# Weight sums of a hybrid block: later stores in the projection, two of twelve groups made in the score stage

## The chip, the cores and the metric

The kernel runs on one core of a Trainium2 chip. The metric is the device time of one execution, in microseconds (us). A core has TensorE (PE, matmuls; its weight loads are PEld), VectorE (DVE), ScalarE (ACT), GpSimd (POOL) and SyncE (SP). Each executes its instructions in the order in which they stand in its own stream, and waits for the others through semaphores. Transfers (DMA) are issued by SyncE, and in one place of this kernel by ScalarE, and run on 16 DMA engines.

## The reference

One layer of a hybrid block on x, 512 tokens of 2048 features in f32:

```python
xn = _rmsnorm(h, norm_mix[l])
y = xn @ w_in[l]
o_gdn = _gdn_group(y[..., :GDN_COLS], ...)      # 8 heads of 128, chunks of 64
o_rwkv = _rwkv_group(y[..., GDN_COLS:], ...)    # 16 heads of 64
mixed = jnp.concatenate([o_gdn, o_rwkv], axis=-1)
h = h + mixed @ w_out[l]
h = h + _cross_attention(_rmsnorm(h, norm_xattn[l]), _rmsnorm(mem, norm_mem[l]),
                         wq, wk, wv, wo)        # 4 heads, 256 memory tokens
hn = _rmsnorm(h, norm_mlp[l])
h = h + jnp.square(jax.nn.relu(hn @ mlp_w_up[l])) @ mlp_w_down[l]   # 2048 -> 8192 -> 2048
return _rmsnorm(h, norm_final)
```

Both recurrent groups solve, for each chunk of 64 tokens, a triangular system (GDN by its formula, RWKV-7 because the kernel computes its scan in chunks too).

## The kernel before, in words

**Stages.** In order: the projection (product tiles py, with the recurrent heads and the key and query products kp and kq of the cross-attention among them) to about 1240 us; the value and output products of the attention (vp, vo) to about 1330; the out projection (op) to 1483; the score stage (sc) to about 1573; the attention's end (at); the MLP's way up (mxu, mgu, mmu) to about 2300; its way down (mxd, mgd, mmd) to the end.

**f32 products.** A weight tile (wraw, w, kqr) of 128x1024 is split into a high part (whi, kqh: a ScalarE cast to a rounded f32) and a low part (wlo, kql: VectorE subtracts). A product is then three matmuls: high x high, high x low, low x high.

**Weight sums.** The MLP multiplies its weights in 2x2 blocks by Strassen-like (Winograd) schemes, which need sums of blocks. Of the down weights w_dm there are 16 groups (e, m); 12 of them (GROUPS) are made beforehand: for each column range, four pieces a21, a22, a11, a12 are loaded, VectorE makes four sums s1 to s4 in place, and each is stored to a DRAM buffer Sd (sd_s in the profile), 2048 columns in all. The MLP loads them from there. `presum` yields these steps for one piece, `presums` goes through the list todo of groups piece by piece, and `ahead` starts it within the projection: NSET = 1 set of four tiles (ds), PIECE = 410 columns, until kp number 15 is done. What is then left in todo, `remaining` and `leftover` make within the MLP, 512 or 256 columns at a time.

**Who sets the order.** The projection and the MLP are ordered by a planner in the kernel's own Python. A chain is a generator that yields operations; each has a rank (`chain(gen, rank)`, the sums' rank is 2 for SyncE and PRANK for the others). `run` takes, again and again, the next operation of the chains by an estimated start (`start`) and the rank, and `issue` emits it: all operations of the planned stages are therefore emitted by one line, L256. A Lane names the engine and carries two numbers of nanoseconds. The first, `wait`, is added to the moment at which the operands are assumed ready, for the operation itself (it is then put later in its engine's stream). The second, `margin`, is added to the assumed landing of the operation's own transfer (whatever uses its result is put later). The lanes of SyncE that matter are SY (none), SL (wait 6000), SM (margin 2500) and the one for the pieces' loads (margin 5000):

```python
SL, SM = Lane(nc.sync, "SP", wait=6000.0), Lane(nc.sync, "SP", margin=2500.0)
t = max(t, x + op[7][0] + (0.0 if by == eng else CROSS))          # start
t, eng = max(state["dma"] + 700, t + 2900) + slack[1], "DMA"      # issue
```

These numbers move nothing at run time; they change only where an instruction stands.

**The triangular inverses.** `rwkv(j)` runs for j = 0 to 7, a pair of RWKV heads each ("head j" from here on), `gdn(h)` for eight GDN heads. Both call `inverse_blocks`: TensorE's products (pg and the like for RWKV, pkk for GDN) are stored to DRAM by SyncE (ndri, ndgi), the 16x16 diagonal blocks are loaded again in another layout (sr, sgi), 33 GpSimd operations invert them (15 steps of two, and copies), the inverses are stored to DRAM (bg16T/bg16U for RWKV, bg8T/bg8U for GDN) and loaded again through the lane SM (r and E for RWKV; gk, gqn for GDN). `inverse_levels` then combines the blocks on TensorE, beginning with the products ri0x to ri7x, or gi0x to gi7x. The small weights lw of `rwkv`, for the product pW, are loaded through SM as well. The matmuls of py that stand between pg (or pkk) and ri_x (or gi_x) in TensorE's stream are called cover below; "wide" is one of 512 columns, "narrow" a smaller one. Other transfers on SyncE in this stage: mixd, gE (from mg and gB), gqd, lg, and the projection's weights, wraw, 512 KB each.

**The score stage.** It, like all that lies between the planned stages, is ordered by the framework's scheduler. A loop over g (2) and n2 (8) makes 16 steps. Each loads two halves of a key tile (kqr, 2 x 256 KB), splits it (kqh, kql; two sets of buffers) and does 24 matmuls of 512 columns on 4 accumulators. In the first six steps `second` makes the high and low parts of the state (hh, hl), `softmax` and `turned` stand between later steps.

Of the kernel before, what the change touches and what calls it, by code (L numbers as in the profile page):

```python
# [9 lines left out]
F32 = mybir.dt.float32  # L10
F32R = mybir.dt.float32r
AF = mybir.ActivationFunctionType
ALU = mybir.AluOpType
# [4 lines left out]
P = 128  # L18
T = 512
M = 256  # L20
# [53 lines left out]
def build(tc, I, out):  # L74
    nc = tc.nc
    V, S, GP, PE = nc.vector, nc.scalar, nc.gpsimd, nc.tensor
# [4 lines left out]
    ps = es.enter_context(tc.tile_pool(name="ps", bufs=1, space=PSUM))  # L81
    pw = es.enter_context(tc.tile_pool(name="pw", bufs=1))
# [45 lines left out]
    def split(src, hi, lo, gain=None):  # L128
        if gain is None:
            S.copy(hi, src)  # L130
            V.tensor_tensor(out=lo, in0=src, in1=hi.bitcast(F32), op=ALU.subtract)  # L131
        else:
            S.activation(hi, src, AF.Copy, scale=gain)
            V.scalar_tensor_tensor(out=lo, in0=src, scalar=gain, in1=hi.bitcast(F32),
                                   op0=ALU.mult, op1=ALU.subtract)

    NWR, NWS, NY = 3, 3, 4
# [66 lines left out]
                return self.key, nm, getattr(self.eng, nm), a, k, out, aps, self.slack  # L204
            return op

    SL, SM = Lane(nc.sync, "SP", wait=6000.0), Lane(nc.sync, "SP", margin=2500.0)
    DV, AC, GS, TE, SY = (Lane(e, k) for e, k in ((V, "DVE"), (S, "ACT"), (GP, "POOL"), (PE, "PE"), (nc.sync, "SP")))

    def cost(op):  # L210
# [142 lines left out]
    KQd = [pd.tile([P, 1024], F32, name=f"kqd{i}", tag=f"kqd{i}") for i in range(16)]  # L353
# [25 lines left out]
    for n in range(2, NIN):  # L379
# [5 lines left out]
    A11, A21, A22, A12 = range(4)  # L385
    Sd = {(e, m, j): pd.tile([P, 2048], F32, name=f"sd{e}_{m}_{j}", tag=f"sd{e}_{m}_{j}")
          for e, m in GROUPS for j in ("s1", "s2", "s3", "s4")}
    NSET, PIECE, PRANK = 1, 410, 5
    todo = list(GROUPS)
    upto = {}  # L390

    def presum(e, m, c, n, d, Q=None):
        Q = Q or SY
        LD = Lane(nc.sync, "SP", margin=5000.0)
        tt = lambda o, a, b, op=ALU.subtract: DV.tensor_tensor(out=o, in0=a, in1=b, op=op)
        src = I["w_dm"][e, m]
        a11, a21, a22, a12 = b = [x[:, 0:n - c] for x in d]
        for i in (A21, A22, A11, A12):
            yield LD.dma_start(b[i], src[i][:, c:n])
        for j, op in (("s1", tt(a22, a21, a22, ALU.add)), ("s3", tt(a21, a11, a21)),  # L400
                      ("s2", tt(a11, a22, a11)), ("s4", tt(a12, a12, a11))):
            yield op
            yield Q.dma_start(Sd[e, m, j][:, c:n], op[5])
            upto[e, m, j] = upto.get((e, m, j), 0) + n - c

    def presums(d, width, stop):
        while todo and not stop():
            e, m = todo.pop(0)
            for c in range(0, 2048, width):
                if c and stop():  # L410
                    todo.insert(0, (e, m))
                    return
                yield from presum(e, m, c, min(c + width, 2048), d)

    hk = [("w", I["wk"][n][:, h * 1024:(h + 1) * 1024]) for n, h in kpo]
    wq += [("m", m) for m in mem4[:3]] + hk[:1] + [("m", mem4[3])] + hk[1:]
# [1146 lines left out]
    def second(n):  # L1563
        hi, lo = act_tile(f"hh{n}"), act_tile(f"hl{n}")
        split(hres[n], hi, lo, col("norm_xattn", n))
        hh_.append(hi)
        hl_.append(lo)
# [66 lines left out]
    def softmax(t):  # L1634
        g, pts, probs = turn[0]
        mx, nb, sm = (pl.tile([P, 2], F32, tag=f"{x}1", name=f"{x}{g}_{t}", bufs=4) for x in ("mx", "nb", "sm"))
        V.tensor_reduce(out=mx, in_=pts[t].rearrange("p (e m) -> p e m", m=M), axis=AX.X, op=ALU.max)
        V.tensor_scalar(out=nb, in0=mx, scalar1=nrcol[:, t:t + 1], scalar2=None, op0=ALU.mult)
        prs = [prob[g * 8 + t * 2 + e][:, 0:M] for e in range(2)]
        for e, pr in enumerate(prs):  # L1640
            S.activation(pr, pts[t][:, e * M:(e + 1) * M], AF.Exp, bias=nb[:, e:e + 1], scale=rcol[:, t:t + 1],
                         accum_out=sm[:, e:e + 1])
        V.reciprocal(out=sm, in_=sm)
        for e, pr in enumerate(prs):
            V.tensor_scalar(out=pr, in0=pr, scalar1=sm[:, e:e + 1], scalar2=None, op0=ALU.mult)
        probs += prs

    def turned():
        g, _, probs = turn.pop(0)
        for e in range(2):  # L1650
            for mt in range(2):
# [4 lines left out]
                S.copy(phi[kk], pt)  # L1656
                V.tensor_tensor(out=plo[kk], in0=pt, in1=phi[kk].bitcast(F32), op=ALU.subtract)

    for g in range(2):
        banks = (("mm", 2), ("mg", 2), ("mg", 2), ("mm", 2)), (("scr", 1), ("scg", 1), ("mx", 2), ("mx", 2))  # L1660
        pts = [psb(f"sc{g}_{t}", *banks[g][t]) for t in range(4)]
        for n2 in range(8):
            cnt[0] += 1
            raw = pw.tile([P, 1024], F32, tag="wraw", name=f"kqr{cnt[0]}", bufs=NWR)
            for i in range(2):
                nc.sync.dma_start(raw[:, i * 512:(i + 1) * 512], KQd[2 * n2 + i][:, g * 512:(g + 1) * 512])
            wh = pw.tile([P, 1024], F32R, tag="whi", name=f"kqh{cnt[0]}", bufs=NWS)
            wl = pw.tile([P, 1024], F32R, tag="wlo", name=f"kql{cnt[0]}", bufs=NWS)
            split(raw, wh, wl)
            if g == 0 and n2 < 6:  # L1670
                second(2 * n2 + 4)
                second(2 * n2 + 5)
            its = [(i, t) for i in range(2) for t in range(4)] if n2 < 7 else [(i, t) for t in range(4) for i in range(2)]
            for i, t in its:
                n = 2 * n2 + i
                w1, w2 = wh[:, i * 512:(i + 1) * 512], wl[:, i * 512:(i + 1) * 512]
                a1, a2 = hh_[n][:, t * P:(t + 1) * P], hl_[n][:, t * P:(t + 1) * P]
                mm(pts[t], a1, w1, start=(n == 0), stop=False)
                mm(pts[t], a1, w2, start=False, stop=False)
                mm(pts[t], a2, w1, start=False, stop=(n == 15))  # L1680
            if g == 0 and n2 == 6:
                norm()
            if g == 1 and n2 < 2:
                softmax(2 * n2)
                softmax(2 * n2 + 1)
            if g == 1 and n2 == 3:
                turned()
        if g == 1:
            for n in range(2):
                begun.append((psb(f"at{n}", "mg"), *wload(VOd[0][:, :, n * P:(n + 1) * P])))  # L1690
                attend(*begun[n], 0)
        turn.append((g, pts, []))
        if g == 1:
            for t in range(4):
                softmax(t)
    turned()

    def alloc(ks):
# [550 lines left out]
    def leftover(left, free, gate, stop=lambda: False, width=512):  # L2249
        r = []  # L2250
        for _ in range(4):
            r.append((yield from take(free)))
        while left and not stop():
            yield lambda: not left or gate(left[0][0] // 2 * 2 + left[0][1])
            if left:
                e, m, c, n = left.pop(0)
                for c in range(c, n, width):
                    yield from presum(e, m, c, min(c + width, n), r, SY)
        free.extend(r)

    wf = []
# [139 lines left out]
```

## Time and profile before

| | us |
|---|---|
| time before, median of 3 runs | 2926.2 |
| lowest and highest of them | 2922.4 and 2928.63 |
| the profiled execution | 2930.33 |
| its span in the trace | 2928.2 |

2.1 us of the profiled execution lie around its span, and it lies 4.1 us above the median. The mean granted clock of TensorE is 0.995 of full speed.

The span in 40 equal slices of 73.2 us; a digit is a busy share in tenths, 9 being 90% or more:

```profile
PE   9999999999999999999999999999999999999998
DVE  7787786786877876769955898888998878787998
ACT  6455554554555655664444655555555644454544
POOL 0213213213212100000000000000000000000000
DMA  5646545555556588685423344655655878888633
```

GpSimd works in the first 14 slices alone, the projection. Slices 20 and 21 (about 1464 to 1610 us) hold the score stage, where DMA shows its smallest shares ahead of the tail. In a row of waits the columns are the engine, what it waited for (tile, line, releaser), the time in all, the number of waits and the longest.

### The profile page before, as it was taken

The numbers are of one execution on the slowest core, as the hardware profiler recorded it, in microseconds if no ns is written. First come the engines' busy times: TensorE is split into PE (matmuls) and PEld (weight loads), VectorE is DVE, ScalarE is ACT, GpSimd is POOL, SyncE is SP. The second block draws the span as 40 slices with busy tenths as digits, with TensorE's granted clock in tenths as the row PEclk, the third lists the DMA queues.
The fourth block names the chain that finished last, engine by engine and source line by source line (L and its number), as shares of the span: only waits on it lengthen the run. The fifth ranks groups of instructions, "written<-read, shape, count | busy, mean of one in ns | idle before, by whom it ended". The sixth has DMA issues, their size and how long they took to land. (4 is left out here: it accounts for less than half of the span.)

```text
span 2928.2 us, 49166 instructions
## 1 busy us (share of the span) xinstructions
PE 2877.8 (98%) x18794; PEld 2422.9 (83%) x18794; DVE 2331.5 (80%) x3551; ACT 1572.7 (54%) x2233; POOL 225.4 (8%) x547
## 2 busy tenths in 40 slices
PE   9999999999999999999999999999999999999998
PEld 7877777777877888879988888888888888888786
DVE  7787786786877876769955898888998878787998
ACT  6455554554555655664444655555555644454544
POOL 0213213213212100000000000000000000000000
PEclk9999999999999999999999999999999999999999
DMA  5646545555556588685423344655655878888633
GB/s 188 176 140 176 152 142 154 159 151 164 156 159 177 180 268 289 217 267 184 130 94 94 108 156 151 199 170 184 196 194 172 295 241 277 292 258 276 198 109 104
DMA packets 315451, 541.47 MB, mean 185 GB/s; under 512 B 101512, under 2 KB 184716, under 8 KB 315216
## 3 DMA queue, kind: packets, MB, share of 16 engines
q1 hardware_dynamic: 288976, 508.97, 56.2%
q10 hardware_dynamic: 26240, 29.37, 2.9%
q8 instruction: 147, 2.41, 0.3%
q14 instruction: 88, 0.72, 0.1%
HBM read 436.11 MB, written 102.12 MB: 184 GB/s over the span
## 5 line engine op out<-in xcount | busy, mean ns | idle before, releaser
L256 ACT CAST whi<-wraw 128x1024 fp32r<-128x1024 f32 (+1 forms) x364 | 381.6, 1049 | 436.8 <-PE py L256 163.2
L256 DVE TENSOR_TENSOR wlo<-wraw,whi 128x1024 fp32r<-128x1024 f32 (+1 forms) x364 | 446.3, 1227 | 114.6 <-ACT whi L256 102.9
L256 PE MATMUL py<-xhi,whi 128*128 128x512 f32 x928 | 374.9, 404 | 6.5 <-ACT xhi L256 6.5
L256 PE MATMUL py<-xlo,whi 128*128 128x512 f32 x928 | 376.4, 406 | 0.0
L256 PE MATMUL py<-xhi,wlo 128*128 128x512 f32 x928 | 374.6, 404 | 0.0
L256 ACT CAST whi<-w 128x1024 fp32r<-128x1024 f32 x181 | 190.5, 1054 | 220.0 <-PE mxu L256 47.3
L256 DVE TENSOR_TENSOR wlo<-w,whi 128x1024 fp32r<-128x1024 f32 x181 | 220.7, 1221 | 50.5 <-ACT whi L256 49.1
L256 PE MATMUL mxu<-cb,whi 128*128 128x512 f32 x1016 | 255.0, 392 | 0.0
L256 PEld LDWEIGHTS py<-xhi,whi 128*128 128x128 f32 x928 | 176.0, 190 | 41.3 <-ACT xhi L256 6.8
L256 PEld LDWEIGHTS mxu<-cb,whi 128*128 128x128 f32 x1016 | 182.8, 189 | 32.7
L256 PEld LDWEIGHTS py<-xlo,whi 128*128 128x128 f32 x928 | 176.0, 190 | 35.8 <-DVE xlo L256 1.4
L256 PEld LDWEIGHTS py<-xhi,wlo 128*128 128x128 f32 x928 | 176.2, 190 | 35.3 <-issue 1.8
L131 DVE TENSOR_TENSOR wlo<-wraw,whi 128x1024 fp32r<-128x1024 f32 x112 | 136.8, 1223 | 46.8 <-ACT whi L130 45.6
L130 ACT CAST whi<-wraw 128x1024 fp32r<-128x1024 f32 x112 | 117.8, 1053 | 88.3 <-PE op L122 25.7
L256 PEld LDWEIGHTS mxu<-cb,wlo 128*128 128x128 f32 x1016 | 138.7, 190 | 10.5 <-DVE wlo L256 0.7
L256 PE MATMUL mxu<-cb,wlo 128*128 128x256 f32 x1016 | 142.2, 282 | 0.3 <-DVE wlo L256 0.3
L256 PE MATMUL mgu<-cb,whi 128*128 128x512 f32 x512 | 129.4, 394 | 1.5 <-ACT whi L256 1.4
L256 PE MATMUL mxd<-whi,cb 128*128 128x512 f32 x512 | 127.0, 390 | 2.6 <-ACT whi L256 2.6
L256 PE MATMUL mgd<-whi,cb 128*128 128x512 f32 x512 | 126.4, 389 | 0.0
L256 ACT ACT_TABLE_LOAD x87 | 111.6, 1283 | 19.3 <-DVE suml_gn L256 11.5
L122 PE MATMUL op<-ob,whi 128*128 128x256 f32 (+1 forms) x752 | 115.3, 304 | 0.2 <-ACT whi L130 0.2
L256 PEld LDWEIGHTS mxd<-whi,cb 128*128 128x128 f32 x512 | 95.8, 188 | 23.7 <-ACT whi L256 3.5
(944 smaller groups left out, 6640.2 us busy)
## 6 DMA issues: line engine op xcount, KB each, us to landing
wraw<-in_w_in SPq DMA_DIRECT2D x116, 512.0 KB, 4.5
wraw<-in_w_up SPq DMA_DIRECT2D x65, 512.0 KB, 3.8
w<-in_w_up SPq DMA_DIRECT2D x63, 512.0 KB, 3.8
w<-sd_s SPq DMA_DIRECT2D x48, 512.0 KB, 5.8
wraw<-sd_s SPq DMA_DIRECT2D x48, 512.0 KB, 5.1
ds<-in_w_dm SPq DMA_DIRECT2D x116, 205.0 KB, 4.1
sd_s<-ds SPq DMA_DIRECT2D x116, 205.0 KB, 4.5
wraw<-in_w_dm SPq DMA_DIRECT2D x46, 512.0 KB, 5.4
```

The lines of the kernel that those rows point to most:

```text
L122: PE.matmul(o, l, r, start=start, stop=stop, skip_group_check=again)
L130: S.copy(hi, src)
L131: V.tensor_tensor(out=lo, in0=src, in1=hi.bitcast(F32), op=ALU.subtract)
L256: f(*a, **k)
```

## The change

Four edits, all about the weight sums and about lanes:

1. SM's margin goes from 2500 to 3500, and PRANK from 5 to 4.
2. In the projection, the stores of sums go through a lane with wait 2000 and margin 2000 (before: SY). The lane of the loads stays. In the MLP both stay as they were.
3. The last two groups of todo, (5, 1) and (5, 0), are taken out of the list ahead of the score stage and made there: 16 steps of 256 columns, step s of the loop making piece s. Two sets (held) of four tiles of 128x256 take turns. The four loads of piece s + 1 are emitted in step s on SyncE (L1664), the four sums on VectorE (L1668 to L1671), and the four stores a step later, on ScalarE's queue (L1677).
4. The load of a key tile is emitted one step ahead (kqload).

Counted in the built programs: in the projection 116 loads, sums and stores each where there were 144 (11880 columns for 14746); in the score stage 64 of each; in the MLP's rest 76 loads and stores each for 92 (8600 columns for 9830). The sum, 24576 columns, is the same.

```diff
                 return self.key, nm, getattr(self.eng, nm), a, k, out, aps, self.slack
             return op
 
-    SL, SM = Lane(nc.sync, "SP", wait=6000.0), Lane(nc.sync, "SP", margin=2500.0)
+    SL, SM = Lane(nc.sync, "SP", wait=6000.0), Lane(nc.sync, "SP", margin=3500.0)
     DV, AC, GS, TE, SY = (Lane(e, k) for e, k in ((V, "DVE"), (S, "ACT"), (GP, "POOL"), (PE, "PE"), (nc.sync, "SP")))
 
     def cost(op):
...
     A11, A21, A22, A12 = range(4)
     Sd = {(e, m, j): pd.tile([P, 2048], F32, name=f"sd{e}_{m}_{j}", tag=f"sd{e}_{m}_{j}")
           for e, m in GROUPS for j in ("s1", "s2", "s3", "s4")}
-    NSET, PIECE, PRANK = 1, 410, 5
+    NSET, PIECE, PRANK = 1, 410, 4
     todo = list(GROUPS)
     upto = {}
 
-    def presum(e, m, c, n, d, Q=None):
-        Q = Q or SY
-        LD = Lane(nc.sync, "SP", margin=5000.0)
+    def presum(e, m, c, n, d, LD=Lane(nc.sync, "SP", margin=5000.0), ST=SY):
         tt = lambda o, a, b, op=ALU.subtract: DV.tensor_tensor(out=o, in0=a, in1=b, op=op)
         src = I["w_dm"][e, m]
         a11, a21, a22, a12 = b = [x[:, 0:n - c] for x in d]
...
         for j, op in (("s1", tt(a22, a21, a22, ALU.add)), ("s3", tt(a21, a11, a21)),
                       ("s2", tt(a11, a22, a11)), ("s4", tt(a12, a12, a11))):
             yield op
-            yield Q.dma_start(Sd[e, m, j][:, c:n], op[5])
+            yield ST.dma_start(Sd[e, m, j][:, c:n], op[5])
             upto[e, m, j] = upto.get((e, m, j), 0) + n - c
 
     def presums(d, width, stop):
...
                 if c and stop():
                     todo.insert(0, (e, m))
                     return
-                yield from presum(e, m, c, min(c + width, 2048), d)
+                yield from presum(e, m, c, min(c + width, 2048), d, Lane(nc.sync, "SP", margin=5000.0), Lane(nc.sync, "SP", 2000.0, 2000.0))
 
     hk = [("w", I["wk"][n][:, h * 1024:(h + 1) * 1024]) for n, h in kpo]
     wq += [("m", m) for m in mem4[:3]] + hk[:1] + [("m", mem4[3])] + hk[1:]
...
                 S.copy(phi[kk], pt)
                 V.tensor_tensor(out=plo[kk], in0=pt, in1=phi[kk].bitcast(F32), op=ALU.subtract)
 
+    early = [(e, m, c) for e, m in (todo.pop() for _ in range(2)) for c in range(0, 2048, M)]
+    held = [[pl.tile([P, M], F32, tag=f"ps{j}{i}", name=f"ps{j}{i}", bufs=1) for i in range(4)] for j in range(2)]
+
+    def early_loads(s):
+        if s < len(early):
+            e, m, c = early[s]
+            for i in (A21, A22, A11, A12):
+                nc.sync.dma_start(held[s % 2][i], I["w_dm"][e, m, i][:, c:c + M])
+
+    def early_sums(s):
+        a11, a21, a22, a12 = held[s % 2]
+        V.tensor_tensor(out=a22, in0=a21, in1=a22, op=ALU.add)
+        V.tensor_tensor(out=a21, in0=a11, in1=a21, op=ALU.subtract)
+        V.tensor_tensor(out=a11, in0=a22, in1=a11, op=ALU.subtract)
+        V.tensor_tensor(out=a12, in0=a12, in1=a11, op=ALU.subtract)
+
+    def early_stores(s):
+        if 0 <= s < len(early):
+            e, m, c = early[s]
+            for i, j in ((A22, "s1"), (A21, "s3"), (A11, "s2"), (A12, "s4")):
+                nc.scalar.dma_start(Sd[e, m, j][:, c:c + M], held[s % 2][i])
+                upto[e, m, j] = c + M
+
+    def kqload(s):
+        raw = pw.tile([P, 1024], F32, tag="wraw", name=f"kqr{s}", bufs=NWR)
+        for i in range(2):
+            nc.sync.dma_start(raw[:, i * 512:(i + 1) * 512], KQd[2 * (s % 8) + i][:, s // 8 * 512:s // 8 * 512 + 512])
+        return raw
+
+    early_loads(0)
+    nextraw = kqload(0)
     for g in range(2):
         banks = (("mm", 2), ("mg", 2), ("mg", 2), ("mm", 2)), (("scr", 1), ("scg", 1), ("mx", 2), ("mx", 2))
         pts = [psb(f"sc{g}_{t}", *banks[g][t]) for t in range(4)]
         for n2 in range(8):
             cnt[0] += 1
-            raw = pw.tile([P, 1024], F32, tag="wraw", name=f"kqr{cnt[0]}", bufs=NWR)
-            for i in range(2):
-                nc.sync.dma_start(raw[:, i * 512:(i + 1) * 512], KQd[2 * n2 + i][:, g * 512:(g + 1) * 512])
+            step = 8 * g + n2
+            raw = nextraw
+            if step < 15:
+                nextraw = kqload(step + 1)
             wh = pw.tile([P, 1024], F32R, tag="whi", name=f"kqh{cnt[0]}", bufs=NWS)
             wl = pw.tile([P, 1024], F32R, tag="wlo", name=f"kql{cnt[0]}", bufs=NWS)
             split(raw, wh, wl)
+            early_stores(step - 1)
+            early_loads(step + 1)
             if g == 0 and n2 < 6:
                 second(2 * n2 + 4)
                 second(2 * n2 + 5)
+            if step < len(early):
+                early_sums(step)
             its = [(i, t) for i in range(2) for t in range(4)] if n2 < 7 else [(i, t) for t in range(4) for i in range(2)]
             for i, t in its:
                 n = 2 * n2 + i
...
         if g == 1:
             for t in range(4):
                 softmax(t)
+    early_stores(15)
     turned()
 
     def alloc(ks):
...
             if left:
                 e, m, c, n = left.pop(0)
                 for c in range(c, n, width):
-                    yield from presum(e, m, c, min(c + width, n), r, SY)
+                    yield from presum(e, m, c, min(c + width, n), r)
         free.extend(r)
 
     wf = []
```

## The prediction

> **What bounds the kernel now.** First the page's span and busy times, then busy time by stage, then TensorE's waits in the projection.
>
> ```profile
> span 2928.2 us, 49166 instructions
> PE 2877.8 (98%) x18794; PEld 2422.9 (83%) x18794; DVE 2331.5 (80%) x3551; ACT 1572.7 (54%) x2233; POOL 225.4 (8%) x547
> ```
>
> TensorE works 2877.8 of 2928.2 us, so all its pauses together are 50.4 us. The change removes and adds no matmul; it can act only on pauses, and on the clock granted after them. Busy time by stretch (from:to, length, PE, PEld, DVE, ACT, POOL, clock, DMA share, GB/s):
>
> ```profile
> 575.00:600.00 25.00, 22.92 (x324) 17.83 (x322) 16.73 (x30) 10.67 (x19) 4.78 (x11) 0.93 0.70 178
> 700.00:725.00 25.00, 24.89 (x309) 19.66 (x308) 15.94 (x29) 11.68 (x19) 11.32 (x31) 0.95 0.59 166
> 925.00:950.00 25.00, 21.45 (x211) 17.23 (x210) 16.45 (x30) 11.39 (x20) 0.00 (x0) 0.86 0.72 211
> 2100.00:2300.00 200.00, 198.58 (x1175) 176.24 (x1174) 178.34 (x235) 113.46 (x160) 0.00 (x0) 1.00 0.60 192
> ```
>
> The MLP (fourth row) pauses 1.4 us in 200, at full clock: making fewer sums there can give nothing. In the projection a pause is followed by a lower clock: 0.93 over 25 us is 1.75 us of work. TensorE's longest waits from 40 to 1050 us:
>
> ```profile
> PE ri6x L256 <- DMA r<-bg16T: 4.2, 2, 3.9
> PE ri2x L256 <- DMA r<-bg16T: 3.2, 2, 3.0
> PE ri5x L256 <- DMA r<-bg16T: 3.1, 2, 2.5
> PE kp L256 <- ACT whi L256: 3.1, 1, 3.1
> PE pW L256 <- DMA lw<-in_w2a: 2.4, 2, 2.1
> PE ri3x L256 <- DMA r<-bg16T: 2.1, 2, 1.6
> PE ri4x L256 <- DMA r<-bg16T: 1.9, 2, 1.5
> SPq L256 <- DVE ds L256: 118.3, 91, 7.2
> ```
>
> Five of the seven are the end of one chain, once per pair of RWKV heads: store to DRAM (ndri), reload (sr), 33 GpSimd operations, store (bg16T), reload (r), then the matmuls ri_x. They sum to 14.5 us. The last row is SyncE: it stood 118.3 us at stores that wait for weight sums, in front of whatever follows, sr and r included.
>
> **Part 1: the projection.** Five edits with one answer: sum stores get 2000 wait and 2000 margin, SM's margin goes from 2500 to 3500, PRANK from 5 to 4, and 28 of 144 loads, sums and stores go. Two spots show what SyncE's order does to sr (start, duration, what; in brackets the idle time before and its releaser):
>
> ```profile
> 666.39 0.60 SPq L256 DMA_DIRECT2D ndri<-GB  x1
> 669.23 0.40 SPq L256 DMA_DIRECT2D wraw<-in_w_in  x1
> 669.74 0.60 SPq L256 DMA_DIRECT2D sr<-ndri  x1
> 678.14 0.21 POOL L256 TENSOR_TENSOR sr<-sr 64x15 f32<-64x15 f32 x1 [27.59 <-DMA sr<-ndri]
> ...
> 213.34 0.60 SPq L256 DMA_DIRECT2D sr<-ndri  x1
> 216.09 0.21 POOL L256 TENSOR_TENSOR sr<-sr 64x15 f32<-64x15 f32 x1 [19.46 <-DVE wlo L256]
> ```
>
> In head 5 a sums load, mixd, gE, gqd and a 512 KB weight load stand between ndri and sr; GpSimd starts 8.40 us after sr is issued. In head 1, where nothing large stands there, it is 2.75. In the changed order only one sum store stands there in heads 3 and 5, so up to 5.65 us come off, more than the waits of ri5x (3.1) and ri3x (2.1): both vanish. What is late next there is nothing: the reload r then lands ahead of its matmuls.
>
> The sums also act through GpSimd, which slows beside a two-input VectorE operation:
>
> ```profile
> 567.00 0.32 POOL L256 TENSOR_TENSOR sr<-sr,sr 64x64 f32<-64x64 f32 x1
> 567.40 1.16 POOL L256 TENSOR_TENSOR sr<-sr 64x63 f32<-64x63 f32 x1
> 567.03 1.38 DVE L256 TENSOR_TENSOR wlo<-wraw,whi 128x1024 fp32r<-128x1024 f32 x1 [0.69 <-ACT whi L256]
> L256 DVE TENSOR_TENSOR ds<-ds,ds x140: 567/580/2149, 105.9 to 1044.4; 128x410 f32<-128x410 f32 x112, 128x408 f32<-128x408 f32 x28
> ```
>
> 0.32 becomes 1.16, so of a 0.58 us sum some 0.4 us is lost to GpSimd. In VectorE's order the sums inside this chain go from 8, 8, 5, 5, 8, 5, 7, 7 (heads 0 to 7) to 7, 5, 5, 5, 4, 4, 4, 4. Head 4: four fewer are 1.6 us of its wait of 1.9, and a split ndri store goes ahead; but three sums loads now stand beside the weight load in front of sr. I take its wait as gone. Head 2: same sums, the weight load still in front of sr; between GpSimd's end and r two small loads replace two stores that waited for sums: -0.7. Head 6: three sums fewer (-1.2) and 12 more wide matmuls as cover (0.23 each below, -2.7), against a 512 KB load now ahead of sr and four more issues ahead of r (about +4): unchanged. Head 7 stays covered. Sum of these waits: -2.1 - 3.1 - 1.9 - 0.7 = -7.8. The wait for lw (2.4; SM's larger margin issues it earlier) I count at -2. kp's 3.1 us stays: its weight load still stands behind r and E.
>
> **A new wait.** The planner now puts the GDN head's product pkk some 24 wide matmuls after ri_x, where it followed within 9. Its inversion ends in gk's reload, then gi_x:
>
> ```profile
> 847.68 1.26 SPq L256 DMA_DIRECT2D gk<-bg8T  x2
> gk<-bg8T SPq DMA_DIRECT2D x3, 64.0 KB, 2.3
> 848.67 0.33 PE L256 MATMUL rs<-BK,BTz 128*128 128x64 f32 x2
> 848.81 0.48 PE L256 MATMUL py<-xhi,whi 128*128 128x512 f32 x1
> 850.05 0.39 PE L256 MATMUL py<-xhi,wlo 128*128 128x512 f32 x1
> 850.28 0.39 PE L256 MATMUL py<-xhi,whi 128*128 128x512 f32 x1
> 857.23 0.27 PE L256 MATMUL gi6x<-gk,gEs 64*64 64x64 f32 x2
> ...
> 382.89 1.26 SPq L256 DMA_DIRECT2D gk<-bg8T  x2
> L256 PEld LDWEIGHTS gi2x<-gk,gEs x16: 129/134/135, 391.5 to 396.3; 64*64 64x64 f32 x16
> ```
>
> By starts, a wide matmul takes 0.23 us (850.05 to 850.28), a narrow one 0.07 (two in 848.67 to 848.81). Slack of gi6x: gk is issued by 848.94, lands 2.3 later at 851.2, used at 857.2: 6.0 us. Between pkk and gi6x the changed order has 25 wide and 48 narrow matmuls fewer: 5.7 + 3.4 = 9.1, so a wait of 3.1 appears. gi2x: 384.15 + 2.3 = 386.5 against 391.5, slack 5.0; it loses 3 wide and 80 narrow, 6.3: a wait of 1.3. Together +4.4, used as +4; bounds 0 (the inversion also loses sums beside it) and +9.1 (no slack).
>
> **The clock.** Heads 4 and 5 have 0.93 and 0.95 after their waits (1.75 and 1.25 us); one new GDN wait would cost 1.75 again. Net -1.5. *What the Trainium skill makes of this:* the 575 row has 2.08 us of pauses in all and still 0.93. "TensorE: Matmul & The Clock Gate" (What's actually happening) gives the half clock as the state after an idle window of about 3.4 us. The trace disagrees with so long a window here; by the rule this term would be 0 and the time 1.5 us later.
>
> Projection: -7.8 - 2 + 4 - 1.5 = -7.3. Bounds: the listed ri, lw and clock losses all gone give -14.5 - 2.4 - 3.0 = -19.9; none gone and the GDN waits at their full size +9.
>
> **Part 2: two groups move to the score stage.** They bring 64 loads, 64 sums and 64 stores of 128 KB there, in two sets of buffers.
>
> ```profile
> 1483.46 0.40 PE L122 MATMUL sc<-kqh,hh 128*128 128x512 f32 x1
> 1506.53 1.22 DVE L131 TENSOR_TENSOR kql<-kqr,kqh 128x1024 fp32r<-128x1024 f32 x1 [4.17 <-ACT kqh L130]
> 1511.97 1.23 DVE L131 TENSOR_TENSOR kql<-kqr,kqh 128x1024 fp32r<-128x1024 f32 x1 [4.22 <-ACT kqh L130]
> kqr<-kqd SPq DMA_DIRECT2D x32, 256.0 KB, 3.1
> DMA packets 5048, 9.55 MB, mean 99 GB/s; under 512 B 560, under 2 KB 560, under 8 KB 5040
> h<-in_w_dm SPq DMA_DIRECT2D x4, 128.0 KB, 4.8
> kqd<-y SPq DMA_DIRECT2D x32, 256.0 KB, 5.5
> ```
>
> A step takes 5.44 us (1506.53 to 1511.97); VectorE is idle 4.2 us of it. Four sums of 256 columns, at 0.58 x 256/410 = 0.36 each, are 1.4 us: hidden. ScalarE's four issues, at the 0.33 of the projection's sum stores, hide in its own idle time. What is not safe is the order: VectorE has 12 of the 16 sets of sums ahead of kql of step 9, six uses of each buffer, and ScalarE puts their stores ahead of its kqh casts. TensorE wants step 9 at 1483.46 + 9 x 5.44 = 1532.4. The first pair of sets is done about 1487 (behind the kql of step 2), so 1487 + 5C + 1.2 must be below 1532.4: C, a buffer's cycle, at most 8.8 us. C is a store's landing, a load's landing, and between them a sum, a store issue, a load issue, half a kqh cast and half a kql: about 0.4 + 0.33 + 0.38 + 0.5 + 0.6 = 2.2. So the landing may be 3.3. Bounds: 3.1 us (kqr, twice the size, at the stage's 99 GB/s) gives C 8.4 and 0; 5.5 (kqd) gives 13.2 and 5 x 4.4 = +22. With the moved 16.8 MB in 87 us the stage carries some 290 GB/s, where 128 KB landed in 4.8 us among 512 KB loads. I take 3.3, nearer to kqr's row: half its size, and nothing above 256 KB in front. Term: 0.
>
> *A rule against it:* the ScalarE queue does not make the stores free. "DMA: Bandwidth & Descriptors" (Issuing engines are not separate DMA queues) says that transfers from every issuing engine interleave on the same 16 DMA engines. Then the landing would be the 4.8 of the loaded row, C 11.8, and +15; no row of before has ScalarE stores beside such loads.
>
> MLP: 16 loads and stores fewer, under a TensorE that doesn't pause: 0.
>
> **Sum.** 2928.2 - 7.3 + 0 = 2920.9 of span, 2923.0 with the 2.1 us around it. The profiled execution was 4.1 above the median of 2926.2: forecast 2919.
>
> **Rivals.** (1) Slower: the score stage runs at the pace of the early buffers. At a landing of 4.8 kql of step 9 is 15 us late, at 5.5 it is 22; with the projection's -7.3, +8 to +15: 2934 to 2941. It decides from a landing of 4.7 (+14, net +6.5). For it: the rate of 290 GB/s and only two sets. Against: two thirds of VectorE's step are idle, and transfers are small. (2) The pauses only move: GDN's new waits reach +9 and head 4 keeps 1.9, so -0.4 net: 2926. For it: shorter cover in GDN heads 2 and 6. Against: fewer sums beside their GpSimd work. (3) Nearly all goes, lower clock included: -19.9, 2906. Against: heads 2 and 6 keep the weight load in front of sr.
>
> **How the numbers follow.** Forecast 0.42, rival 1 0.30, rival 2 0.18, rival 3 0.10. This kernel's measurement tells 0.2% (5.9 us) from no change. Faster takes the forecast but for 0.02, and rival 3: 0.50; same takes most of rival 2, and 0.03 more: 0.18; slower takes rival 1 and the tail of rival 2: 0.32. The forecast's own range, GDN waits from 0 without their lower clock (-5.75) to +9 (+5), is 2913 to 2924; a landing of 3.7 (+4) stays inside. The 8-in-10 range reaches past rival 3 and into rival 1's: 2903 to 2939.
>
> **What would show it.** Right: waits of ri3x, ri4x, ri5x under 0.5 us; GpSimd's first operation under 4 us after sr's issue in heads 3 and 5; gi2x and gi6x waiting 1 to 4 us; score steps at 5.44. Wrong: sc waiting on kql about step 9 and 128 KB landings above 4 us; GDN waits above 9; ri6x growing.

## The result and the profile after

The changed kernel takes 2944.0 us (median of 6 runs) against 2928.6 for before in the same comparison: ratio 1.0052, 95% interval 1.0037 to 1.0067 (a ratio above 1 is slower than before). It is slower, where a gain was forecast. One of the twelve executions of e15 below took 8656.55 us; its ratio goes without it, and no trace of e15 is read.

The page of the changed kernel, its span, the busy times, and by slices of 73.7 us the busy tenths of PE and the DMA share:

```profile
span 2946.2 us, 49322 instructions
PE 2886.0 (98%) x18794; PEld 2428.0 (82%) x18794; DVE 2331.4 (79%) x3571; ACT 1573.2 (53%) x2233; POOL 231.8 (8%) x547
PE   9999999999999999999989999999999999999998
DMA  5645546546556678784484344555565868876633
```

The matmuls are the same 18794. Their busy time is 8.2 us longer (2886.0 for 2877.8), which is lower clock, and the pauses are 60.2 us for 50.4. In slice 20 (1473 to 1547 us) the DMA share is 8 where it was 2: the moved sums. There, too, PE shows its only 8 before the tail.

Where the 18.0 us between the two profiled spans lie (the medians differ by 15.4) is read from the first start of each stage's products (groups of one tile; count: shortest/median/longest in ns, first and last start). Before:

```profile
L122 PE MATMUL sc<-kqh,hh x128: 388/389/486, 1483.5 to 1572.7; 128*128 128x512 f32 x128
L122 PE MATMUL at<-phi,whi x128: 389/389/497, 1573.4 to 1662.2; 128*128 128x512 f32 x128
L256 PE MATMUL mxd<-whi,cb x512: 388/389/501, 2300.7 to 2875.3; 128*128 128x512 f32 x171
```

and after:

```profile
L122 PE MATMUL sc<-kqh,hh x128: 388/389/794, 1476.6 to 1587.6; 128*128 128x512 f32 x128
L122 PE MATMUL at<-phi,whi x128: 389/389/499, 1588.2 to 1677.1; 128*128 128x512 f32 x128
L256 PE MATMUL mxd<-whi,cb x512: 387/389/637, 2317.5 to 2893.2; 128*128 128x512 f32 x171
```

The score stage starts 6.9 us earlier. These are single profiles: over all runs the stage starts between 1467.8 and 1479.0 us in nine profiles with the new projection, and between 1481.7 and 1490.0 in four with the old. From its first product to the first of at it takes 111.6 us for 89.9: +21.7. From there to mxd 729.3 for 727.3, and mxd to the end 628.7 for 627.5: +2.0 and +1.2. The sum is +18.0. "The stage" below is this length, 89.9 before.

TensorE's waits in the stage, and its busy time there (length, PE, PEld, DVE, ACT, POOL, clock, DMA share, GB/s):

```profile
PE ptr L1652 <- DVE plo L1655: 6.0, 1, 6.0
PE sc L122 <- ACT rcol L125: 3.8, 1, 3.8
PE sc L122 <- DVE kql L131: 2.1, 2, 1.3
PE sc L122 <- ACT kqh L130: 1.8, 1, 1.8
...
1476.00:1588.00 112.00, 98.18 (x414) 79.52 (x413) 61.65 (x124) 33.85 (x54) 0.00 (x0) 0.92 0.70 218
```

13.8 us are pauses; the clock of 0.92 makes the other 8 of the 21.7. All four releasers are ordinary work of the stage (the transposes' low part, the norm's scale, the key tile's two halves): each stood late in its own stream. What stood in front of it is seen on VectorE and ScalarE (start, duration, operation, idle time before and its releaser):

```profile
1473.10 0.42 DVE L1668 TENSOR_TENSOR ps<-ps,ps 128x256 f32<-128x256 f32 x1
...
1529.55 0.42 DVE L1668 TENSOR_TENSOR ps<-ps,ps 128x256 f32<-128x256 f32 x1 [1.19 <-DMA ps<-in_w_dm]
...
1536.74 1.21 DVE L131 TENSOR_TENSOR kql<-kqr,kqh 128x1024 fp32r<-128x1024 f32 x1
...
1523.94 1.04 ACT L130 CAST kqh<-kqr 128x1024 fp32r<-128x1024 f32 x1 [8.88 <-DMA sd_s<-ps]
1524.94 6.98 ACTq L1677 DMA_DIRECT2D sd_s<-ps  x6
1531.95 1.28 ACT L125 ACT_TABLE_LOAD   x1 [6.97 <-DMA sd_s<-ps]
...
1539.85 0.40 PE L122 MATMUL sc<-kqh,hh 128*128 128x512 f32 x1
```

The first two rows are the first sums of pieces 0 and 11. For piece 11 VectorE waits 1.19 us at a load, in front of kql; ScalarE stands seven microseconds at six stores, and the table load for the norm's scale follows them. kql of step 9 starts at 1536.74, when TensorE, undisturbed, would have wanted it at 1476.6 + 9 x 5.44 = 1525.6. But TensorE doesn't stop at this kql. Its waits for kqh, kql and rcol all lie in steps 7 and 8 (a step is 24 matmuls; step 8 starts at 1525.04, and the last row is the first matmul of step 9). It reaches step 9 at 1539.85, some 14 us late already, and finds kql done at 1537.95. The two longest of these waits, kqh (1.8) and rcol (3.8), come from ScalarE: kqh of step 8 and the table load each stand behind a row of stores.

In the projection TensorE's waits from 40 to 1060 us are:

```profile
PE ri6x L256 <- ACT gE L256: 7.0, 1, 7.0
PE ri7t L256 <- DVE k L256: 4.6, 1, 4.6
PE ri4x L256 <- DMA r<-bg16T: 3.2, 2, 2.8
PE ri2x L256 <- DMA r<-bg16T: 1.4, 2, 1.0
```

The waits of ri3x, ri5x, pW and kp are gone; ri4x and ri6x wait longer, and ri7t is new. The row of ri6x names gE, but the product reads r and GA: what it waited for is r, as head 6 below shows.

### The profile page after: what moved, and what is told of

Same layout as the page of the kernel before. It is cut to its first block, busy times and chain, and to the rows that moved or that the text cites. A ratio compares the mean times of both kernels' runs of the same rounds, so it can differ in the third digit from the quotient of the medians.

```text
span 2946.2 us, 49322 instructions
## 1 busy us (share of the span) xinstructions
PE 2886.0 (98%) x18794; PEld 2428.0 (82%) x18794; DVE 2331.4 (79%) x3571; ACT 1573.2 (53%) x2233; POOL 231.8 (8%) x547
## 4 chain that ended last, share of the span: by engine, by line
PE 85%; DMA 7%; DVE 3%; POOL 2%; ACT 1%; issue 1%; SPq 0%; ACTq 0%; DVEq 0%; POOLq 0%
PE py L256 18%; PE mxu L256 12%; PE mgu L256 6%; PE mgd L256 6%; PE mxd L256 6%; PE op L122 5%; PE kp L256 3%; PE vp L122 3%; PE at L122 3%; PE scrd L256 3%; PE scgd L256 3%; PE mmu L256 3%; PE mmd L256 3%; PE kq L256 2%; POOL sr L256 2%
## 5 line engine op out<-in xcount | busy, mean ns | idle before, releaser
L256 PEld LDWEIGHTS mxu<-cb,wlo 128*128 128x128 f32 x1016 | 138.7, 190 | 10.5 <-DVE wlo L256 0.7
L256 ACT ACT_TABLE_LOAD x87 | 111.6, 1283 | 19.8 <-DVE suml_gn L256 9.9
```

The source lines that it names most:

```text
L256: f(*a, **k)
```

## The experiments

Each is compared with before in 5 rounds on the same chip. Theory after the result: the stage loses because the streams of VectorE and ScalarE put the pieces ahead of the stage's own work faster than two buffer sets deliver them. Rivals: the traffic of 290 GB/s costs by itself; the loss belongs to the projection's new order; the eight transfers that the program allows in flight limit the pieces.

**e1, the projection's edits alone.** The score stage of before is put back; what is left in todo falls to the MLP.

```diff
-    early = [(e, m, c) for e, m in (todo.pop() for _ in range(2)) for c in range(0, 2048, M)]
...
-            early_stores(step - 1)
-            early_loads(step + 1)
```

> The projection's edits alone (SM's margin, PRANK, the lane of the sum stores); the score stage as before, and what the projection leaves over is made in the MLP, 4096 columns more than in the changed kernel. Theory: the projection's gain of 6.9 us stands by itself and the whole loss is the score stage's: score stage back at 89.6 us, time 5 to 8 us below before (ratio 0.9973 to 0.9983). Rival: the MLP can't take the extra sums for nothing, its stage grows by 5 us or more and the time is that of before or above.

Measured: 2965.3 us, ratio 1.0129 (1.0114 to 1.0145). The stage is back at 89.9 and starts at 1473.3, 10 us earlier than before; but mxd to the end takes 672.8 us for 627.5. So the rival is right: the MLP can't take the extra 4096 columns. Its longest wait there, and a stretch of the chain that ended last (start, duration, what):

```profile
PE mxd L256 <- ACT whi L256: 25.8, 3, 23.2
...
2618.72 0.61 DVE sl L256
2619.35 2.44 DMA sd_s<-sl
2622.24 3.79 DMA sl<-in_w_dm
...
2635.86 2.55 DMA sd_s<-sl
2639.33 5.93 DMA w<-sd_s
```

Load, sum, store, load, one after another in one set of tiles, and at the end the MLP's own load of the sum. The two parts of the change belong together: fewer sums in the projection have to be made somewhere before the way down.

**e2, the score stage alone.** The three edits of the projection undone:

```diff
-    ... Lane(nc.sync, "SP", margin=3500.0)
+    ... Lane(nc.sync, "SP", margin=2500.0)
-    NSET, PIECE, PRANK = 1, 410, 4
+    NSET, PIECE, PRANK = 1, 410, 5
-    ..., Lane(nc.sync, "SP", margin=5000.0), Lane(nc.sync, "SP", 2000.0, 2000.0))
+    ...)
```

> The two groups in the score stage and the earlier key tile loads, with the lanes and PRANK of before. Theory: start of the score stage as before (1483 us), the stage 20 to 23 us longer (before 89.6), ratio 1.007 to 1.008. Rival: the loss hangs together with the projection's new order; then the stage is less than 15 us longer.

Measured: 2947.8, ratio 1.0068 (1.0055 to 1.0080). The stage starts at 1482.1 and takes 107.8 us: +17.9, a little below the expected +20 to +23, and above the rival's bound. The loss is the stage's own.

**e3, one group in the score stage.** Eight pieces, at the same rate while they last.

```diff
-    early = [... for e, m in (todo.pop() for _ in range(2)) ...]
+    early = [... for e, m in (todo.pop() for _ in range(1)) ...]
```

> The changed kernel with one group, 8 pieces, in the score stage. The transfers run at the same rate while they last. Theory (VectorE's order puts more sets of sums ahead of a kql than two buffer sets of 10.3 us a cycle deliver): 8 pieces are done 6.8 + 6 x 5.15 = 37.7 us after the stage's start, kql of step 7 is wanted at 38.1, so 1 to 3 us are lost and the stage takes 91 to 93 us; time 3 to 6 us below before. Rival (the traffic costs by its bytes, through the key tiles' landing): half of 21.8, so the stage takes 100 us and the time is 4 us above before.

Measured: the stage takes 90.0 us, where the theory had 91 to 93: nothing lost, with the earlier key tile loads in place. The first sums of its 8 pieces run from 1470.4 to 1507.7, one each 5.3 us. The total is 2946.1 (1.0061), as mxd to the end takes 650.3: the group that went back to the MLP costs there 22.8, half of e1's 45.3. Not a line of this was in the expectation, which looked at the stage alone.

**e4, one piece a step.** All 16 pieces, tied in issue order: the sums of piece s stand behind kql of step s + 1, its stores behind kqh of step s + 2, and two pieces are loaded ahead of the stage.

```diff
-            split(raw, wh, wl)
-            early_stores(step - 1)
-            early_loads(step + 1)
+            kh = S.copy(wh, raw)
+            kl = V.tensor_tensor(out=wl, in0=raw, in1=wh.bitcast(F32), op=ALU.subtract)
+            with tc.issue_after(kh.ins):
+                early_stores(step - 2)
+            if step > 1:
+                early_loads(step)
...
-            if step < len(early):
-                early_sums(step)
+            if step > 0:
+                with tc.issue_after(kl.ins):
+                    early_sums(step - 1)
```

> The changed kernel with the same 16 pieces and bytes, but the order in the streams tied: the sums of piece s stand behind kql of step s + 1 on VectorE, its stores behind kqh of step s + 2 on ScalarE. Theory: a set's cycle of 10.3 us fits two steps (10.9 us), so no kql or kqh waits for a piece; the stage takes 89.6 to 92 us and the time is 4 to 8 us below before. Rival (the traffic itself): kqr lands late or the pieces still block, the stage is at least 10 us longer than before's and the time at or above before.

Measured: 2926.7, ratio 1.0001 (0.9992 to 1.0010). The transfers and bytes are those of the changed kernel, and so are the landings (median us in the last column; first the changed kernel from 1470 to 1595 us, then e4 from 1475 to 1575):

```profile
sd_s<-ps ACTq DMA_DIRECT2D x64, 128.0 KB, 3.8
ps<-in_w_dm SPq DMA_DIRECT2D x56, 128.0 KB, 3.2
kqr<-kqd SPq DMA_DIRECT2D x26, 256.0 KB, 4.6
```

```profile
sd_s<-ps ACTq DMA_DIRECT2D x64, 128.0 KB, 3.5
ps<-in_w_dm SPq DMA_DIRECT2D x56, 128.0 KB, 3.5
kqr<-kqd SPq DMA_DIRECT2D x26, 256.0 KB, 4.3
PE ptr L1652 <- DVE plo L1655: 2.2, 2, 1.1
```

The stage takes 94.1 us, above the expected 92, but 17.5 of the 21.7 go by order alone. No sc product waits any more; the rest is the last row, the transposes of the first half's probabilities, whose low part stands behind the sums of piece 11.

**e5, plo ahead of the sums.** The sums of piece 11 behind plo of the first half, those of pieces 14 and 15 behind plo of the second.

```diff
-            if g == 1 and n2 == 3:
-                turned()
+            if g == 1 and n2 == 3:
+                last = turned()
...
+            if step == 12:
+                kh, kl = last
```

> As e4_one_piece_a_step, and plo of the first half's probabilities stands ahead of the sums of piece 11, those of the second half ahead of pieces 14 and 15. Theory: what e4 still lost (94.1 us for the stage, 2.2 us of it in the transposes that wait for plo, the rest lower clock behind them) goes: stage 90 to 91.5 us, time 3 to 5 us below e4, so 0.9985 of before. Rival (the 290 GB/s themselves cost the last 4 us, for instance through late kqr): the stage stays at 93 us or more.

Measured: the stage is 89.9 us, as long as before, at 250 GB/s for 98 and with 14.7 of the moved 16.8 MB issued inside it. That settles the traffic's rival. But the time is 2927.7 (0.9996; 0.9987 to 1.0005): from at to the MLP's first product 94.9 us for 89.5. ScalarE, near the stage's end and behind it:

```profile
1552.86 7.91 ACTq L1678 DMA_DIRECT2D sd_s<-ps  x8
1560.86 2.00 ACT L130 CAST whi<-wraw 128x1024 fp32r<-128x1024 f32 x2 [10.42 <-DMA sd_s<-ps]
...
1576.10 4.08 ACTq L1678 DMA_DIRECT2D sd_s<-ps  x8
```

Eight stores (pieces 12 and 13) hold ScalarE for 7.9 us although the last of their sums is done at 1556.7; the releaser is a landing. In the built program each store waits for its sum and for an earlier transfer on one of eight semaphores that all transfers share; the trace doesn't say which of these it was. The eight stores at 1576.10 (pieces 14 and 15) hold it for 4.1 us more, and the largest pause of this part comes behind them: from 1584.5 to 1589.5 us TensorE works 3.15 of 5.00. e9 and e10 tell the two rows apart.

**e6, e4 with the old projection.** The same three lines as in e2, on e4.

> e4_one_piece_a_step with the lanes and PRANK of before in the projection. Theory: the projection's edits are worth 5 to 7 us by themselves, so this is 5 to 7 us slower than e4: 1.002 of before. Rival: they are worth nothing beyond the scatter of single profiles (start of the stage between 1473 and 1479 us in four kernels with the same projection), and this stands within 2 us of e4.

Measured: 2936.7, ratio 1.0038 (1.0024 to 1.0052), 10 us above e4. Its stage takes 97.7 us for e4's 94.1 (the transposes wait 5.1 us), so some 6.4 of the 10 are the projection's. The split is rough: the profiled execution of e6 lies 9.2 us above its median.

**e7, the stores on SyncE.**

```diff
-                nc.scalar.dma_start(Sd[e, m, j][:, c:c + M], held[s % 2][i])
+                nc.sync.dma_start(Sd[e, m, j][:, c:c + M], held[s % 2][i])
```

> The changed kernel with the stores of the 16 pieces issued by SyncE. ScalarE's casts then stand behind no store, and VectorE has 9 pieces ahead of kql of step 9 where it had 12. Theory (pieces delivered each 5.15 us from 6.8 us after the stage's start): the ninth is done at 48, kql then at 49.2, wanted at 49.0: the stage takes 90 to 93 us. Rival (SyncE, which now waits for sums and landings ahead of key tile loads, becomes the wait): stage over 96 us, with TensorE's waits traced to kqr.

Measured: 2934.8, ratio 1.0015 (1.0004 to 1.0026), stage 103.3 us: a miss. sc waits 0.7 us in all, where it waited 7.7: without the stores in its stream ScalarE delays no sc product. But one wait that the count left out takes the place:

```profile
PE ptr L1652 <- DVE plo L1655: 9.5, 1, 9.5
```

plo had later pieces in front of it here. Neither theory's waits at kqr nor a free stage: the same cause, sums ahead of ready work, at another place.

**e8, merged loads.** The four loads of a piece as one of 512 KB, so 7 transfers a step for 10.

```diff
-            for i in (A21, A22, A11, A12):
-                nc.sync.dma_start(held[s % 2][i], I["w_dm"][e, m, i][:, c:c + M])
+            nc.sync.dma_start(whole_[s % 2], I["w_dm"][e, m][:, :, c:c + M].rearrange("i p c -> p i c"))
```

> The changed kernel with each piece's four loads made as one transfer of 512 KB (16 instead of 64). In the program every transfer also waits for the one eight issues before it on its semaphore lane; the changed kernel has 10 transfers a step, this has 7. VectorE has 9 pieces ahead of kql of step 9 (12 before). Theory A (the cycle of the two buffers limits: landing of a store, then of a load): the pieces come no faster than each 5.1 us where they wait for nothing else, the stage takes 91 to 95 us because fewer stand ahead. Theory B (the eight lanes limit): the pieces come each 4.6 us or faster and the stage takes about 90 us. Either way below the changed kernel's 111.6 us.

Measured: 2938.2, ratio 1.0033 (1.0020 to 1.0046), stage 105.1. First sums of pieces 0 and 11:

```profile
1473.94 0.42 DVE L1668 TENSOR_TENSOR ps<-ps 128x256 f32<-128x256 f32 x1
...
1543.09 0.43 DVE L1668 TENSOR_TENSOR ps<-ps 128x256 f32<-128x256 f32 x1 [4.86 <-DMA ps<-in_w_dm]
```

69.15 / 11 = 6.3 us a piece, slower than the changed kernel's 5.1 over the same pieces with more transfers. So the number in flight alone doesn't pace the pieces. The run changes two more things, though: a set must be free as a whole before it is loaded, and its load of 512 KB lands in 5.3 us where the 128 KB took 3.2 (the stores in 2.7 for 3.8). (Stage and time missed the expected numbers of both theories: again the wait is plo, 8.7 us.)

**e9, merged loads with e5's order.**

> e5_plo_ahead with the merged loads. In e5 the stage was back at 89.9 us but the attention's end took 94.9 for 89.5: ScalarE stood 10.4 us at stores that wait for earlier transfers of their lanes, ahead of a weight cast. Theory: with 7 transfers a step for 10 these waits shrink, the attention's end takes 90 to 92 us and the time is 3 to 5 us below e5 (ratio 0.998). Rival: the stores wait for their sums, not for lanes; then it stays at 94 us.

Measured: 2927.1, ratio 0.9990 (0.9981 to 0.9999); stage 89.9, at to the MLP 93.9. The rival is nearer: fewer transfers took off 1.0 of 5.4 us, and TensorE's largest pause still comes behind the stores of pieces 14 and 15.

**e10, the last stores on SyncE.** Only those of pieces 14 and 15, in e9.

```diff
     last = turned()
     for s in (14, 15):
         with tc.issue_after(last[1]):
             early_sums(s)
-        with tc.issue_after(last[0]):
-            early_stores(s)
+        early_stores(s, nc.sync)
```

> e9_merged_plo_ahead with the stores of pieces 14 and 15 on SyncE: in e9 they stood on ScalarE ahead of the weight casts of the attention's end, which took 93.9 us for 89.5. Theory: both stages at 89.5 to 90.5 us, so what is left is the projection's gain: 4 to 7 us below before, ratio 0.9975 to 0.9987. Rival: the sums of these pieces on VectorE are what delays the attention's end; it stays at 93 us or more and the ratio at 0.999.

Measured: 2921.1, ratio 0.9971 (0.9960 to 0.9982). It beats both kernels. Stage 89.9, at to the MLP 89.5, so the stores of these two pieces made what e9 still lost:

```profile
L122 PE MATMUL sc<-kqh,hh x128: 387/389/486, 1472.6 to 1561.8; 128*128 128x512 f32 x128
L122 PE MATMUL at<-phi,whi x128: 387/389/496, 1562.5 to 1651.4; 128*128 128x512 f32 x128
```

**e11 to e15: which edit of the projection pays.** All have e10's score stage. e11: margin back at 2500. e12: the old lane of the stores. e13: PRANK back at 5. e14: all three. e15: PRANK 4 as the only edit.

> e10 with SM's margin back at 2500. Theory: the margin only brings lw and r forward by one place or so, worth the 2.4 us of lw's wait: 0.0005 to 0.001 above e10. Rival: the margin is the main edit of the three, and 4 us or more come back.

> e10 with the sum stores of the projection in their old lane (no wait, no margin). Theory: the stores that wait for sums in front of sr and r are the main cause of the projection's pauses, so 4 to 6 us come back: the waits of ri3x and ri5x above 2 us again, 0.0015 to 0.002 above e10. Rival: the number of pieces and their place (PRANK, margin) matter and the lane doesn't: within 0.0005 of e10.

> e10 with PRANK back at 5; margin 3500 and the lane stay; the projection makes 27 pieces. If PRANK carries the projection's gain: 5 to 7 us above e10, ratio about 0.9992. If the fewer pieces or any new order does: within 0.001 of e10.

> e10's score stage with all three edits of the projection undone (36 pieces). Sizes the projection's gain without a stage that loses: theory 5 to 8 us above e10 (0.999 to 1.0 of before). If the score stage still loses against this projection the spans by stage show it.

> e10's score stage with PRANK 4 as the only edit of the projection (41 pieces made there). If PRANK carries the gain: ratio 0.996 to 0.9975, as e10 to e12. If it takes any two of the three: between that and e14.

| | margin | stores' lane | PRANK | pieces | us | ratio to before, 95% |
|---|---|---|---|---|---|---|
| e10 | 3500 | new | 4 | 29 | 2921.1 | 0.9971 (0.9960 to 0.9982) |
| e11 | 2500 | new | 4 | 29 | 2918.7 | 0.9966 (0.9953 to 0.9979) |
| e12 | 3500 | old | 4 | 41 | 2919.9 | 0.9966 (0.9953 to 0.9979) |
| e13 | 3500 | new | 5 | 27 | 2918.3 | 0.9963 (0.9946 to 0.9979) |
| e15 | 2500 | old | 4 | 41 | 2922.5 | 0.9974 (0.9964 to 0.9984) |
| e14 | 2500 | old | 5 | 36 | 2928.4 | 0.9999 (0.9986 to 1.0012) |

e14 sizes the projection's gain: 0.9999 - 0.9971 = 0.28%, 8.2 us; each of the two ratios is known to some 0.12%. No one of the three edits is needed; whichever is undone, the gain stays, and PRANK alone brings it (e15). The theories of e11 and e12, by which some of it comes back, missed. The margin alone and the lane alone were not run. TensorE's waits in the projection of e12, where the stores are back in the old lane and 12 more pieces are made than in e10:

```profile
PE pW L256 <- DMA lw<-in_w2a: 4.9, 3, 2.5
...
SPq L256 <- DVE ds L256: 120.8, 98, 7.9
```

SyncE waits 120.8 us for sums, as before (118.3), and still no product ri_x waits more than 0.3 us. In e14 they are back: ri6x 5.8, ri5x 3.3, ri2x 2.6, ri4x 2.1. All of TensorE's waits of 0.2 us and more in the projection sum to 23 us in before and in e14, and to 12 to 20 in e10 to e13, at other products each time. What the other orders have in common, that the old one lacks, was not found; it stays open.

## Why the prediction was wrong, step by step

**The step that failed: the score stage's term, 0.** The inequality named the right cause, pieces ahead of the stage's own work, with inputs that were too small. It asked that a buffer's cycle C be at most 8.8 us, took a landing of 3.3 and 2.2 us beside it, and saw C at 8.8, on the edge. Measured: the first sums of pieces 0 and 11 start at 1473.10 and 1529.55, so 5.13 us a piece and C = 10.3. The landings are 3.8 (stores) and 3.2 (loads), 0.4 above the assumption together; the rest of the cycle is 3.3 for 2.2. And the first pair was done at 1483.4, 6.8 us after the stage's start where 3.5 were assumed. By the inequality: 6.8 + 5 x 10.3 + 1.2 = 59.5 against 49.0, 10.5 us late. Most of this is the rest of the cycle (5 x 1.1) and the later start (3.3); the landings give 5 x 0.4 = 2.0. The trace has 1536.74 + 1.2 - 1525.6 = 12.3, of which 2.2 are VectorE's wait for rcol. e3 tests it from one side (eight pieces fit: 90.0 us), e4 and e5 from the other (the same bytes, tied: 94.1 and 89.9).

**Three things that the term left out.** It priced VectorE's stream alone. That ScalarE puts the stores ahead of its kqh casts was written down, and not priced; kqh of step 8 and rcol stood there, and with kql of steps 7 and 8 they had stopped TensorE for 7.7 us before step 9 was reached. So the stage did run at the pace of the buffers, but the place of the loss was another than the kql that the sum looked at, and the agreement of 10.5 and 12.3 is in part luck. Second, it stopped at step 9. The longest wait, 6.0 us of 13.8, is the transposes' plo, which stood behind later pieces; in e7 and e8 it is the only large one. And it priced stalls at their length: the lower clock behind them cost another 8 us. Together they brought the stage to +21.7, rival 1's upper end (+22), though its landing (3.5, not 4.8 to 5.5) was not what rival 1 had: by its sum a landing of 3.5 gives +2. The time, 15.4 us above before, lies at the end of its +8 to +15.

**Why the landing was on the wrong side.** The bound with 290 GB/s was written down, with 4.8 us (that row was taken at 272 GB/s), and the value was taken near the row of an idle stage. The stage then moved 218 GB/s on average, stalls included, and the two landings came to 3.5 on average: little above 3.3, but with the threshold at the assumed value nothing was left for error. The rule of the Trainium skill that was weighed there, "DMA: Bandwidth & Descriptors" (Issuing engines are not separate DMA queues: they interleave on the same 16 DMA engines), spoke for a longer landing. The trace agrees in direction: kqr, still issued by SyncE, landed in 4.6 us where it had 3.1, with the stores on ScalarE. How much of this is the issuing engine no run shows: with the same stores on SyncE (e7) it landed in 3.7.

**The projection's term, -7.3, was right in size** (-6.9 at the stage's start in the profile, 8.2 by e14 and e10) and half right in its steps. Head 5 as predicted: GpSimd starts 2.80 us after sr is issued (8.40 before):

```profile
661.18 0.59 SPq L256 DMA_DIRECT2D sr<-ndri  x1
...
663.98 0.21 POOL L256 TENSOR_TENSOR sr<-sr 64x15 f32<-64x15 f32 x1 [18.72 <-DMA sr<-ndri]
```

ri3x, ri5x and pW are free. Head 4 was wrong: the weight load and three sums loads that stand beside sr were seen and passed over; GpSimd starts 7.9 us after sr, and ri4x waits 3.2 for 1.9 before. Head 6 was expected at 4.2 and is 7.2. The sum had set one more load ahead of sr and four issues ahead of r at some 4 us together. r alone loses more: it is issued at 799.51, 4.5 us after the store bg16T, where it was 2.8, and it lands 8.8 us after that, where it was 5.0. The loads of gE and gqd and a 512 KB weight load stand in front of it; before, it was a weight load and one sums load.

```profile
r<-bg16T SPq DMA_DIRECT2D x2, 128.0 KB, 8.8
808.40 0.44 PE L256 MATMUL ri6x<-r,GA 64*64 64x64 f32 x2 [6.96 <-ACT gE L256]
```

The operation on gE that the last row names ended 0.1 us ahead of it, at about the landing of r; in e10, with the same projection, the same wait is put down to r (8.2 us). kp's wait went (3.6 us, forecast to stay), ri7t's 4.6 came (not foreseen), and the GDN waits (+4.4) did not come. For gi6x the cover shrank by 7.9 us, about as counted (9.1), but the chain from pkk to gk's landing shrank too, from 32.6 to 27.8 us, which the sum had put at nothing. So the total is right by errors that cancel, which is luck, and its reason fell: e12 has the old lane, more sums, the same waits of SyncE for them, and the gain.

**The clock rule.** By the page of the Trainium skill "TensorE: Matmul & The Clock Gate" (What's actually happening) half clock needs an idle window of about 3.4 us. In the changed kernel the long waits agree (3.8 us for rcol, in ten microseconds at 0.66; 6.0 us for plo, in ten at 0.67). The trace of before, with 0.93 in a stretch of 2.1 us of pauses, doesn't, nor does the changed kernel from 1520 to 1530 us: 0.83, with the matmuls slow from 1526.3 on, behind waits of 1.8 and 0.8 us and ahead of the long one. No run here settles it.

**The MLP's term, 0,** holds for the change (+2.0 and +1.2). What it hid is e1's 45 us: the two groups could not have gone there.

## What to carry to other kernels

Where a scheduler fixes the order of an engine's stream, work that waits for transfers must be issued no faster than its buffers come round: compare the cycle of a buffer with the rate at which the order uses it, on every engine that has the pieces in its stream, and for every later instruction that stands behind, not the first alone. A cycle that sits on the threshold is no forecast of "nothing": 1.5 us more of it, with a start 3.3 us later, was enough for a loss of 21.7, and e4 and e5 show that tying one piece to each step takes that back with the same traffic. And a gain that appears with a new order isn't shown to come from the edit that was meant to bring it until that edit alone is undone.

## What the runs showed of the hardware, not expected

With the DMA share at 0.85 to 0.91 the stage loses nothing when no ready work stands behind a transfer: in e4 TensorE has no pause from 1490 to 1540 us. Two stretches of ten microseconds:

```profile
1500.00:1510.00 10.00, 10.00 (x46) 8.29 (x45) 5.58 (x10) 2.10 (x2) 0.00 (x0) 1.00 0.91 281
1540.00:1550.00 10.00, 8.96 (x46) 7.23 (x45) 6.27 (x11) 3.17 (x4) 0.00 (x0) 1.00 0.95 304
```

The second holds 1.0 us of pause, one of the two waits for plo. And 128 KB stores on ScalarE's queue and 128 KB loads on SyncE's landed in 3.5 us each in e4, where 128 KB loads among 512 KB ones took 4.8 in the MLP of before, at a share of 0.82. That looks like a landing that goes by the size of the transfers in front, but e8 and e9 speak against it: there, too, 512 KB loads run beside them, and the 128 KB stores landed in 2.7 and 3.3 us. What sets the landing stays open.
